# Attention's values by token in four banks, and the fourth tile of the norm turned one step earlier, in a hybrid decoder layer

## The chip, the cores and the metric

One core of a Trainium2 chip runs the whole layer in one launch. The metric is the device time of that launch in microseconds (us). The kernel before was run three times: 647.14, 649.06 and 649.33 us, median 649.06. A further, profiled execution took 649.91 us.

## The reference, cut to what matters

A decoder layer on 512 tokens of width 1024, all in fp32. The input is normed and projected; eight heads of block-sparse attention and eight heads of a chunked delta rule (GDN) run side by side on the projections; both are joined, projected out, normed and added, and a squared-ReLU MLP follows, again normed and added.

```python
h = rms_norm(x, pre_mix_norm[l])
proj = jnp.einsum('bsd,dc->bsc', h, w_in[l])
att_q, att_k, att_v, gdn_qkv, gdn_z, gdn_a, gdn_b = jnp.split(proj, split_points, axis=-1)
o_att = moba_attention(att_q, att_k, att_v, rel_bias)
o_gdn = gated_deltanet(gdn_qkv, gdn_z, gdn_a, gdn_b, ...)
mix = jnp.einsum('bsc,cd->bsd', jnp.concatenate([o_att, o_gdn], axis=-1), w_out[l])
x = x + rms_norm(mix, post_mix_norm[l])
h = rms_norm(x, pre_mlp_norm[l])
m = jnp.einsum('bsf,fd->bsd', jnp.square(jax.nn.relu(jnp.einsum('bsd,df->bsf', h, w_up[l]))), w_down[l])
x = x + rms_norm(m, post_mlp_norm[l])
```

With 512 tokens and blocks of 256, all earlier blocks are selected, so attention is causal softmax over all keys, with a bias by distance.

## The kernel before, in words

**Precision.** Each large product is made as three matmuls of operands split into a high and a low part (`mm3`, L139): high by high, high by low, low by high. The split is a rounding copy on ScalarE and a subtraction on VectorE or GpSimd. Scores times values, the GDN scan and all turns are plain fp32.

**The projections** (`projections`, L247) have 28 items of 128 output columns, in the order of the string `ORDER` (L26): k, q, v, z are GDN's, x, y, w are attention's queries, keys and values of one pair of heads. An item is 8 steps of `mm3` into a bank of the tag `mm` (there are two): weights stand still, the normed input `hT` (features by tokens) moves, 512 columns a matmul. So a result lies with its columns on the partitions and tokens along the free axis. After the last step a stream (`take_k`, `take_q`, `take_v`, `take_z`, `take_a`) takes the bank away. For a value item (`ev_v`, L625) that is a ScalarE copy out of the bank (L627), four turns of 128x128 on TensorE into a bank of the tag `a` (L629, by the helper L83) and a second ScalarE copy (L631), because scores times values wants tokens on the partitions. Weights come in halves of an item, 256 KB each, on SP's queue, two halves ahead.

**The order of the work.** TensorE's order is written by the kernel itself. `Weave` (L29) holds streams, Python generators with a rank. It keeps a clock of its own, `weave.now`, that each matmul advances by a modelled time, and always goes on with the stream of lowest rank that is due. A stream yields either a delay (from the table `WAIT`, L20, in modelled us) or the name of a mark that another stream sets. The projections (rank 5) yield after each `mm3` and so fill what the others leave. On the other engines a list scheduler sets the order by its own model; `LEAD` (L23) is a head start there. On TensorE nothing overtakes: if a matmul's operand is late, all waits.

**Attention** is done by pairs of heads, p = 0 to 3. `scores` (L645) waits for the mark `a{p}` and, after the first pair, for `turned{p-1}`; for four blocks of queries it makes two score banks (tag `a`, of which there are three), VectorE adds the bias and takes the minimum (L669), ScalarE takes the exponential (L671). `values` (L681) turns the probabilities and multiplies them with the pair's values; its last step (L727) scales, and the mark `att{p}` follows. Items x2 and x3 wait for `att0` and `att1`.

**GDN.** `chunks` (L554) makes the matrices of a pair of heads from k and q: `turned` (L512) builds the tile RC (L525 to L527), which `rows` spreads by matmuls. `inverse` (L732) then solves 32x32 triangles on VectorE alone: 31 rounds of a product (L743) and a subtraction (L744). `scan` (rank 3) runs the recurrence once `inverse` and v0 to v3 are done.

**The output** (`output`, L936) multiplies by w_out for four tiles of 128 tokens; the steps of pair 3 come in `second` (needs `att3`). `normed` (L979), one stream a tile, sums squares on ScalarE, scales and adds on VectorE (L992, L993, L998), waits `WAIT["normed"]`, turns the tile in two banks of the tag `a` and splits it (L112, L113). `up0` (rank 7) then multiplies the first columns of w_up, four parts for tokens 0 to 255, waits for `n3`, and four parts for tokens 256 to 511.

**After that** up and down are made with fewer, combined products and a written-out order on all engines. Nothing there is touched.

Large tiles come from the pool `big` with 14 slots; scratch of attention from `at`.

Of the kernel before, what the change touches and what calls it, by code (L numbers as in the profile page):

```python
# [28 lines left out]

class Weave:  # L30
# [35 lines left out]
                self.live.remove(s)  # L66


def layer(ctx, tc, nc, x, w_in, w_ab, w_out, w_up, w_down, conv_w, a_log, dt_bias, gdn_norm_w, rel_bias,
          pre_mix, post_mix, pre_mlp, post_mlp, c_ident, c_mask, c_tri, c_ones, c_sel, c_su, c_hot, out):  # L70
    stt = nc.vector.scalar_tensor_tensor
    tt = nc.vector.tensor_tensor
# [84 lines left out]
    def bank(tag="g", shape=(128, 512)):  # L157
        return psum.tile(list(shape), FT, name="ps_" + tag, tag=tag, bufs={"mm": 2, "g": 3, "a": 3}[tag])
# [7 lines left out]
    def kof(pair, k, cols=slice(0, 512)):  # L166
        return pair[k // 4][:, k % 4, cols]
# [92 lines left out]
    def projections(items):  # L260
        begin = lambda n, at=None: begun(w_in[items[n // 2][0] // 128, :, 4 * (n % 2):4 * (n % 2) + 4], (4, 128), at)
        end = lambda w: ended(w, nc.gpsimd.tensor_tensor)
        load = lambda n: end(begin(n))
        W = first_w
        W += [begin(0), begin(1)]
        yield 0
        w1 = big("w1", dt=FR)
        W += [begin(2 + i, (w1[:, 2 * i], w1[:, 2 * i + 1], nb0[:, 1024 + 512 * i:1536 + 512 * i])) for i in range(2)]
        yield 0
        for i in range(2):  # L270
            W[i] = end(W[i])
# [18 lines left out]
        W = [third, load(5)]  # L290
        for n in range(4, 2 * len(items)):
            col, ev, need = items[n // 2]
            if n % 2 == 0:
                if need:
                    yield need
                ps = bank("mm")
            if n + 2 < 2 * len(items):
                W.append(load(n + 2))
            hi, lo = W.pop(0)
            for j in range(4):  # L300
                k = 4 * (n % 2) + j
                mm3(ps, hi[:, j], lo[:, j], kof(hT_h, k), kof(hT_l, k), k == 0, k == 7)
# [311 lines left out]
    def take_a(p):  # L614
        def ev_q(ps):
            pts[p] = big("pt", dt=FR)
            nc.scalar.mul(pts[p][:, 0], ps, -0.125)
            stt(pts[p][:, 1], ps, -0.125, f32(pts[p][:, 0]), op0=OP.mult, op1=OP.subtract)
            yield 0

        def ev_k(ps):
            split(pts[p][:, 2], pts[p][:, 3], ps)
            yield 0

        def ev_v(ps):  # L625
# [9 lines left out]
        return [(128 * p, ev_q, need), (512 + 128 * p, ev_k, None), (1024 + 128 * p, ev_v, None)]  # L635

# [6 lines left out]
    def scores():  # L643
        for p in range(4):
# [257 lines left out]
    W = {}  # L902
# [78 lines left out]
    def normed(t, P, xs, nb):  # L981
# [48 lines left out]
    def up0():  # L1030
# [458 lines left out]
```

## Time and profile before

| | us |
|---|---|
| median of three runs | 649.06 |
| the profiled execution | 649.91 |
| its span, first to last instruction | 648.1 |
| outside the span | 1.8 |
| TensorE busy | 630.9 |
| VectorE busy | 443.8 |
| ScalarE busy | 361.5 |
| GpSimd busy | 180.6 |

Times in the rows are us from the span's start; "x4" counts merged instructions; what stands in brackets behind a row is idle time of the engine just before, and what ended it. The mean of "one" is its time in the pipeline; the next matmul can start before it ends, so the distance from start to start is what a matmul costs. The stages: norm and first items to about 30 us, projections with GDN and attention to about 270, output product to 320, up to about 490, down to the end.

### The profile page before, as it was taken

The page shows a single profiled execution, that of the slowest core. Times are in us where ns is not written, and L with a number is a line of the kernel's source. Part 1 is how long each engine was busy: PE and PEld are TensorE (multiplying, and loading weights), DVE is VectorE, ACT ScalarE, POOL GpSimd, SP SyncE. Part 2 cuts the span into 40 slices and gives each one's busy share as a digit, 9 for nine tenths or more (in the row PEclk, how much of TensorE's full clock was granted, in tenths as well). Part 3 has the DMA queues.
Part 4 walks back from the last instruction along what each step waited for, and adds up shares of the span by engine and source line. Part 5 has one row for each costly group of instructions (what it writes and reads, how often), then busy time and mean ns, then how long its engine had stood idle before and what let it go on. Part 6 is the DMA issues. An engine that isn't in the chain of part 4 may idle for free.

```text
span 648.1 us, 11158 instructions
## 1 busy us (share of the span) xinstructions
PE 630.9 (97%) x4375; PEld 527.0 (81%) x4375; DVE 443.8 (68%) x619; ACT 361.5 (56%) x614; POOL 180.6 (28%) x219
## 2 busy tenths in 40 slices
PE   7999999999999999999999999999999999999995
PEld 6877787666777777687898899999998888887884
DVE  5357764898522455665755578787879888988776
ACT  6367645264647556744423476656665656665661
POOL 5356475332446334002402311221211130000002
PEclk7999999989999999999999999999999999999999
DMA  7231223323351113561399899989999999757503
GB/s 239 83 100 66 66 88 95 112 81 114 107 105 51 34 45 105 192 231 73 122 357 247 187 287 226 280 239 261 290 223 342 293 292 293 242 199 296 189 1 129
DMA packets 60341, 113.16 MB, mean 175 GB/s; under 512 B 15702, under 2 KB 34777, under 8 KB 59906
## 3 DMA queue, kind: packets, MB, share of 16 engines
q1 hardware_dynamic: 42594, 83.10, 36.8%
q0 software_dynamic: 17696, 29.36, 21.6%
q8 instruction: 34, 0.56, 0.3%
q14 instruction: 17, 0.14, 0.1%
HBM read 106.65 MB, written 35.15 MB: 219 GB/s over the span
## 4 chain that ended last, share of the span: by engine, by line
PE 84%; DVE 7%; DMA 3%; ACT 2%; POOL 1%; issue 1%; SPq 0%; DVEq 0%; POOLq 0%; ACTq 0%
PE ps_mm L79 42%; PE ps_g L79 24%; PE ps_a L79 15%; PE ps_a L83 2%; DVE conv L364 1%; PE ps_g L83 1%; DVE pr L743 1%; DVE inv L744 1%; DMA xx<-in_x 1%; DMA wd<-d_T 1%; POOL by L174 1%; DMA inv<-d_n 0%; DMA w_raw<-in_w_in 0%; DVE ma_l L113 0%; DMA wo_raw<-in_w_out 0%
## 5 line engine op out<-in xcount | busy, mean ns | idle before, releaser
L137 POOL TENSOR_TENSOR w_lo<-w_raw,w_hi 128x512 fp32r<-128x512 f32 x54 | 70.8, 1311 | 103.1 <-ACT w_hi L136 94.1
L79 PE MATMUL ps_mm<-hT_h,w_hi 128*128 128x512 f32 (+1 forms) x224 | 93.8, 419 | 0.4 <-DVE conv L364 0.4
L79 PE MATMUL ps_mm<-hT_l,w_hi 128*128 128x512 f32 (+1 forms) x224 | 87.5, 391 | 0.4 <-DVE hT_l L113 0.4
L79 PE MATMUL ps_mm<-hT_h,w_lo 128*128 128x512 f32 (+1 forms) x224 | 87.3, 390 | 0.0
L112 ACT CAST wdh<-wd 128x1024 fp32r<-128x1024 f32 x53 | 55.9, 1054 | 52.0 <-PE ps_mm L79 23.5
L113 DVE TENSOR_TENSOR u_l<-w,u_h 128x1024 fp32r<-128x1024 f32 x46 | 56.2, 1224 | 36.0 <-ACT u_h L112 35.4
L113 DVE TENSOR_TENSOR wdl<-wd,wdh 128x1024 fp32r<-128x1024 f32 x53 | 64.9, 1225 | 22.8 <-ACT wdh L112 22.7
L112 ACT CAST u_h<-w 128x1024 fp32r<-128x1024 f32 x46 | 47.8, 1047 | 55.6 <-PE ps_a L79 20.7
L1169 POOL DMA_DIRECT2D d_T<-in_w_down x32 | 33.0, 1032 | 144.7 <-DMA d_T<-in_w_down 73.9
L136 ACT CAST w_hi<-w_raw 128x512 fp32r<-128x512 f32 x56 | 34.6, 619 | 40.0 <-PE ps_mm L79 20.9
L79 PEld LDWEIGHTS ps_mm<-hT_h,w_hi 128*128 128x128 f32 x224 | 43.4, 194 | 13.9 <-issue 6.0
L79 PEld LDWEIGHTS ps_mm<-hT_h,w_lo 128*128 128x128 f32 x224 | 43.5, 194 | 9.0
L170 POOL TENSOR_SCALAR s<-s 128x1 f32<-128x1 f32 x12 | 3.8, 316 | 163.9 <-DVE s L1364 107.7
L79 PEld LDWEIGHTS ps_mm<-hT_l,w_hi 128*128 128x128 f32 x224 | 43.6, 195 | 6.8 <-DVE hT_l L113 0.7
L79 PE MATMUL ps_mm<-wdh,u_h 128*128 128x512 f32 x116 | 45.3, 390 | 0.0
L79 PE MATMUL ps_mm<-wdl,u_h 128*128 128x512 f32 x116 | 45.1, 389 | 0.0
L79 PE MATMUL ps_mm<-wdh,u_l 128*128 128x512 f32 x116 | 45.1, 389 | 0.0
L364 DVE SCALAR_TENSOR_TENSOR conv<-ps_mm,cw,conv 128x511 f32<-128x511 f32 (+2 forms) x36 | 26.8, 744 | 12.6 <-ACT conv L361 12.1
L113 DVE TENSOR_TENSOR u_l<-f,u_h 128x1024 fp32r<-128x1024 f32 x28 | 34.1, 1219 | 0.0
L79 PE MATMUL ps_g<-wdh,u_h 128*128 128x512 f32 x80 | 31.2, 390 | 0.4 <-DVE y L1343 0.4
L79 PE MATMUL ps_g<-wdh,u_l 128*128 128x512 f32 x80 | 31.1, 389 | 0.0
L79 PE MATMUL ps_g<-wdl,u_h 128*128 128x512 f32 x80 | 31.1, 389 | 0.0
(434 smaller groups left out, 1728.4 us busy)
## 6 DMA issues: line engine op xcount, KB each, us to landing
d_T<-in_w_down POOLq DMA_DIRECT2D x48, 512.0 KB, 9.8
wd<-d_T SPq DMA_DIRECT2D x32, 512.0 KB, 6.1
w<-in_w_up SPq DMA_DIRECT2D x28, 512.0 KB, 7.2
w_raw<-in_w_in SPq DMA_DIRECT2D x54, 256.0 KB, 2.6
wd<-in_w_down SPq DMA_DIRECT2D x24, 512.0 KB, 7.5
wo_raw<-in_w_out SPq DMA_DIRECT2D x16, 256.0 KB, 2.9
d_T<-d_T POOLq DMA_DIRECT2D x8, 512.0 KB, 11.9
xx<-in_x SPq DMA_DIRECT2D x4, 512.0 KB, 3.3
```

What stands on the lines that cost most here:

```text
L79: nc.tensor.matmul(o, l, r, **kw)
L83: nc.tensor.transpose(o, i, ident[:k, :k])
L112: nc.scalar.copy(hi, src)
L113: tt(lo, src, f32(hi), op=OP.subtract)
L136: nc.scalar.copy(hi, raw)
L137: (sub or tt)(lo, raw, f32(hi), op=OP.subtract)
L170: nc.gpsimd.tensor_scalar(r, ss, 1.0 / n, EPS, op0=OP.mult, op1=OP.add)
L174: nc.gpsimd.tensor_tensor(r, r, m, op=OP.pow)
L364: stt(c[:, s:], p[:, :512 - s], cw[:, ft, j:j + 1], c[:, s:], op0=OP.mult, op1=OP.add)
L743: tt(v, iN[:, 0:m, m:m + 1].to_broadcast([128, m, w]), iU[:, m:m + 1, m:32].to_broadcast([128, m, w]), op=OP.mult)
L744: tt(iU[:, 0:m, m:32], iU[:, 0:m, m:32], v, op=OP.subtract)
L1169: nc.gpsimd.dma_start(d_T[t][k], block(b, second)[k], accum_op=OP.add, max_dma_last_dim=1024)
```

## The change

- The four value items become one: `by_token` (new). The normed input stands still (128 tokens), the values' weights move (512 columns, all eight heads), for each of 8 steps and 4 tiles of tokens one `mm3`, into four banks, `mm`, `mm`, `a`, `g`. The result has tokens on the partitions, so `ev_v` and its turns go; four ScalarE copies fill one `big` tile `VT`, which `values` reads. The weights come as a new input `w_v` of eight pieces of 128x512, by the same queue and the same distance ahead.
- The mark `a{p}` is set by the keys' item, and `values` waits for a mark `v`.
- `ORDER`: the one value item stands after x1 and ahead of v0 to v3; y0 comes four items earlier.
- `normed` has a delay of its own for tile 3 and a `g` bank for the second half of tile 1.
- `WAIT`, `RANK`, `LEAD` and `START` have other numbers.

```diff
-WAIT = {..., 'k': 4.72, 'q': 3.34, 'z': 7.99, 'r_out': 3.96, 'kk': 1.97, 'va': 1.38, 'a': 2.4, 'row': 1.38, 'rows': 3.2, 'att': 1.43, 'p1': 1.88, 'p2': 1.7, 'w': 1.78, 'state': 1.12, 'normed': 11.21, ...}
-RANK = {'chunks': 5, 'inverse': 3, 'scan': 3, 'scores': 5, 'values': 5, 'finish_o': 1, 'take': 4}
-LEAD = {'chunks': 0, 'inverse': 0, 'scan': 100, 'scores': 0, 'values': 100, 'finish_o': 400, 'take': 0, 'take_a': 100}
+WAIT = {..., 'k': 5.19, 'q': 2.1, 'z': 2.87, 'r_out': 4.94, 'kk': 2.44, 'va': 0.5, 'a': 5.28, 'row0': 1.24, 'row': 1.38, 'rows': 5.12, 'att': 1.17, 'p1': 2.8, 'p2': 0.82, 'w': 2.33, 'state': 1.23, 'normed3': 7.6, 'normed': 8.97, ...}
+RANK = {'chunks': 1, 'inverse': 3, 'scan': 3, 'scores': 5, 'values': 5, 'finish_o': 2, 'take': 3}
+LEAD = {'chunks': 0, 'inverse': 100, 'scan': 100, 'scores': 0, 'values': 100, 'finish_o': 0, 'take': 200, 'take_a': 100}
-START = (5.5, 9.0, 17, 16, 33, 10.5)
-ORDER = "k0 q0 x0 k1 k2 q1 q2 k3 z0 q3 y0 x1 v0 w0 v1 y1 w1 v2 v3 x2 y2 w2 x3 y3 z1 w3 z2 z3"
+START = (5.5, 9.0, 17, 16, 30, 16.5)
+ORDER = "k0 q0 x0 k1 q1 q2 y0 k2 k3 z0 q3 x1 w0 v0 v1 v2 v3 y1 x2 y2 x3 y3 z1 z2 z3"
+V_BANKS = "mm mm a g"
...
+    def by_token(W, u, ahead):
+        VT.append(big("V"))
+        ps = [bank(t) for t in V_BANKS.split()]
+        for k in range(8):
+            ahead(u + k)
+            hi, lo = W[u + k]
+            for t in range(4):
+                ts = slice(128 * t, 128 * t + 128)
+                mm3(ps[t], kof(hT_h, k, ts), kof(hT_l, k, ts), hi[:, 0], lo[:, 0], k == 0, k == 7)
+                if k == 7:
+                    nc.scalar.copy(VT[0][:, t], ps[t])
+                yield 0
+        mark("v", WAIT["va"])
...
         def ev_k(ps):
             split(pts[p][:, 2], pts[p][:, 3], ps)
+            mark(f"a{p}", WAIT["a"])
             yield 0
-        def ev_v(ps):
-            v = at.tile([128, 512], FT, name="t2")
-            nc.scalar.copy(v, ps)
-            yield WAIT["va"]
-            tp = transposed(by_tile(v), "a")
-            vals[p] = at.tile([128, 512], FT, name="V")
-            nc.scalar.copy(vals[p], tp)
-            mark(f"a{p}", WAIT["a"])
...
-                yield WAIT["row"]
+                yield WAIT["row" if p else "row0"]
...
             yield f"row{p}3"
-            V = vals[p].rearrange("p (t h e) -> p t h e", t=4, h=2)
+            yield "v"
...
-        yield WAIT["normed"]
+        yield WAIT["normed" if t < 3 else "normed3"]
         for b in range(2):
-            tp = bank("a")
+            tp = bank("g" if t == b == 1 else "a")
```

## Rows read from the trace of the kernel before

**Rows 1.** The page's first part: engine, busy us (share of the span), instructions

```profile
PE 630.9 (97%) x4375; PEld 527.0 (81%) x4375; DVE 443.8 (68%) x619; ACT 361.5 (56%) x614; POOL 180.6 (28%) x219
```

**Rows 2.** Who waited for whom, TensorE: us in total, times, longest

```profile
PE ps_a L79 <- DVE mins L669: 1.8, 1, 1.8
...
PE ps_g L79 <- DVE ssq L382: 0.9, 1, 0.9
PE ps_g L83 <- ACT sqt L378: 0.7, 1, 0.7
...
PE ps_g L79 <- DVE RC L527: 0.5, 1, 0.5
```

**Rows 3.** Windows after the longest wait: busy and count by engine, PEclk, DMA, GB/s

```profile
130.00:132.00 2.00, 1.52 (x6) 1.09 (x7) 2.00 (x8) 1.54 (x4) 0.14 (x1) 0.59 0.02 4
132.00:134.00 2.00, 2.00 (x6) 1.57 (x7) 2.00 (x5) 1.14 (x4) 1.14 (x1) 0.56 0.00 0
```

**Rows 4.** Groups of instructions that go: busy us, mean ns, idle before

```profile
L83 PE MATMUL ps_a<-ident,t 128*128 128x128 f32 x16 | 2.6, 283 | 0.0
...
L631 ACT COPY V<-ps_a 128x512 f32<-128x512 f32 x4 | 2.3, 587 | 3.3 <-PE ps_a L83 3.3
```

**Rows 5.** Timeline of TensorE around four of those turns: start, us, instruction

```profile
153.53 0.66 PE L83 MATMUL ps_a<-ident,t 128*128 128x128 f32 x4
153.94 0.48 PE L79 MATMUL ps_mm<-hT_h,w_hi 128*128 128x512 f32 x1
154.25 0.39 PE L79 MATMUL ps_mm<-hT_l,w_hi 128*128 128x512 f32 x1
```

**Rows 6.** Timeline of TensorE where the down product changes its bank

```profile
510.99 0.39 PE L79 MATMUL ps_g<-wdh,u_l 128*128 128x512 f32 x1
511.22 0.39 PE L79 MATMUL ps_a<-wdh,u_h 128*128 128x512 f32 x1
```

**Rows 7.** The window of those changes, columns as in rows 3

```profile
510.00:520.00 10.00, 10.00 (x46) 8.29 (x45) 8.56 (x8) 6.86 (x8) 3.06 (x4) 1.00 1.01 243
```

**Rows 8.** Timeline at the end of item x1: its last matmul and its two readers

```profile
108.83 0.39 PE L79 MATMUL ps_mm<-hT_h,w_lo 128*128 128x512 f32 x1
...
109.60 0.59 ACT L617 ACTIVATE pt<-ps_mm 128x512 fp32r<-128x512 f32 x1
...
110.22 0.69 DVE L618 SCALAR_TENSOR_TENSOR pt<-ps_mm,pt 128x512 fp32r<-128x512 f32 x1 [1.16 <-ACT pt L617]
```

**Rows 9.** A window among the convolutions, columns as in rows 3

```profile
60.00:80.00 20.00, 18.42 (x118) 14.59 (x116) 15.09 (x27) 13.26 (x36) 8.98 (x11) 1.00 0.25 66
```

**Rows 10.** Group of the widest score operations on VectorE: busy us, mean ns, idle before

```profile
L669 DVE CUSTOM_DVE_ANT_0 L<-ps_a,E 128x512 f32<-128x512 f32 x8 | 5.3, 688 | 14.5 <-PE ps_a L79 14.5
```

**Rows 11.** Timeline of TensorE at the norm's turns and the first up product

```profile
307.35 0.66 PE L83 MATMUL ps_a<-ident,xs 128*128 128x128 f32 x4 [0.59 <-DVE ma_l L113]
...
318.76 0.28 PE L79 MATMUL ps_mm<-ma_h,wu 128*128 128x256 f32 x1
...
331.13 1.04 PE L83 MATMUL ps_a<-ident,xs 128*128 128x128 f32 x8
332.41 0.38 PE L79 MATMUL ps_mm<-ma_h,wu 128*128 128x256 f32 x1 [0.24 <-ACT ma_h L112]
333.13 0.39 PE L79 MATMUL ps_mm<-ma_l,wu 128*128 128x256 f32 x1 [0.34 <-DVE ma_l L113]
```

**Rows 12.** Timeline of VectorE in the norm of tile 2

```profile
311.69 3.58 DVE L137 TENSOR_TENSOR w_lo<-w_raw,w_hi 128x512 fp32r<-128x512 f32 x2 [0.32 <-ACT w_hi L136]
...
318.59 1.28 DVE L998 SCALAR_TENSOR_TENSOR xs<-xs,s,nb 128x1024 f32<-128x1024 f32 x1 [2.19 <-POOL s L174]
```

**Rows 13.** Timeline of TensorE: pair 3's first scores, and where pair 3 is needed

```profile
252.47 0.96 PE L79 MATMUL ps_a<-pt 64*128 64x512 f32 x6
...
291.68 0.39 PE L79 MATMUL ps_mm<-wo_h,ma_h 128*128 128x512 f32 x1
```

**Rows 14.** The pairs' last step on VectorE: ns min/median/max, first and last start

```profile
L727 DVE TENSOR_TENSOR t<-ps_a,t x4: 683/688/692, 154.7 to 275.6; 128x512 f32<-128x512 f32 x4
```

More of the change, by code (lines that the diff above doesn't have):

```diff
@@ L18 @@
 EPS = 1e-6
-WAIT = {'h': 1.7, 'conv_k': 5.5, 'k': 4.72, 'conv_q': 6.15, 'q': 3.34, 'conv_v': 11.0, 'v': 6.02, 'z': 7.99, 'ab': 0.1, 'g': 11.93, 'scalars': 4.6, 'r_in': 0.72, 'r_out': 3.96, 'kk': 1.97, 'kk_out': 14.43, 'gl': 2.12, 'qk': 4.27, 'va': 1.38, 'a': 2.4, 'row': 1.38, 'rows': 3.2, 'pv': 1.54, 'att': 1.43, 'inverse': 0.9, 'merge': 11.0, 'p1': 1.88, 'p2': 1.7, 'w': 1.78, 'vn': 1.0, 'state': 1.12, 'o_in': 3.6, 'o': 3.73, 'wo': 0.88, 'wo_out': 17.6, 'normed': 11.21, 'n': 1.7, 'up': 1.9, 'sums': 1.5, 'turned': 0.5, 'pv0': 1.5}
-RANK = {'chunks': 5, 'inverse': 3, 'scan': 3, 'scores': 5, 'values': 5, 'finish_o': 1, 'take': 4}
-LEAD = {'chunks': 0, 'inverse': 0, 'scan': 100, 'scores': 0, 'values': 100, 'finish_o': 400, 'take': 0, 'take_a': 100}
+WAIT = {'h': 1.7, 'conv_k': 5.5, 'k': 5.19, 'conv_q': 6.15, 'q': 2.1, 'conv_v': 11.0, 'v': 6.02, 'z': 2.87, 'ab': 0.1, 'g': 11.93, 'scalars': 4.76, 'r_in': 0.72, 'r_out': 4.94, 'kk': 2.44, 'kk_out': 14.43, 'gl': 2.75, 'qk': 3.88, 'va': 0.5, 'a': 5.28, 'row0': 1.24, 'row': 1.38, 'rows': 5.12, 'pv': 1.54, 'att': 1.17, 'inverse': 0.9, 'merge': 11.0, 'p1': 2.8, 'p2': 0.82, 'w': 2.33, 'vn': 1.0, 'state': 1.23, 'o_in': 3.6, 'o': 3.73, 'wo': 0.97, 'wo_out': 17.6, 'normed3': 7.6, 'normed': 8.97, 'n': 2.12, 'up': 1.9, 'sums': 1.5, 'turned': 0.5, 'pv0': 1.53}
+RANK = {'chunks': 1, 'inverse': 3, 'scan': 3, 'scores': 5, 'values': 5, 'finish_o': 2, 'take': 3}
+LEAD = {'chunks': 0, 'inverse': 100, 'scan': 100, 'scores': 0, 'values': 100, 'finish_o': 0, 'take': 200, 'take_a': 100}
 FILL = (6, 2)
 AT_X = (3, 5)
-START = (5.5, 9.0, 17, 16, 33, 10.5)
-ORDER = "k0 q0 x0 k1 k2 q1 q2 k3 z0 q3 y0 x1 v0 w0 v1 y1 w1 v2 v3 x2 y2 w2 x3 y3 z1 w3 z2 z3"
+START = (5.5, 9.0, 17, 16, 30, 16.5)
+ORDER = "k0 q0 x0 k1 q1 q2 y0 k2 k3 z0 q3 x1 w0 v0 v1 v2 v3 y1 x2 y2 x3 y3 z1 z2 z3"
+V_BANKS = "mm mm a g"
 class Weave:
@@ L66, in run, with layer @@
                 self.live.remove(s)
-def layer(ctx, tc, nc, x, w_in, w_ab, w_out, w_up, w_down, conv_w, a_log, dt_bias, gdn_norm_w, rel_bias,
+def layer(ctx, tc, nc, x, w_in, w_v, w_ab, w_out, w_up, w_down, conv_w, a_log, dt_bias, gdn_norm_w, rel_bias,
           pre_mix, post_mix, pre_mlp, post_mlp, c_ident, c_mask, c_tri, c_ones, c_sel, c_su, c_hot, out):
@@ L289, in projections, with ahead @@
                 yield 0
[L290 to L302, printed above, removed]
+        units = [(i, m) for i in range(2, len(items)) for m in range(2 if items[i] else 8)]
+        W = [third]
+        def ahead(u):
+            while len(W) < min(len(units), u + 3):
+                i, m = units[len(W)]
+                W.append(load(2 * i + m) if items[i] else wchunk(w_v[m], (1, 512), nc.gpsimd.tensor_tensor))
+        u = 0
+        ahead(-1)
+        for item in items[2:]:
+            if not item:
+                yield from by_token(W, u, ahead)
+                u += 8
+                continue
+            col, ev, need = item
+            if need:
+                yield need
+            ps = bank("mm")
+            for k in range(8):
+                if k % 4 == 0:
+                    ahead(u + k // 4)
+                hi, lo = W[u + k // 4]
+                mm3(ps, hi[:, k % 4], lo[:, k % 4], kof(hT_h, k), kof(hT_l, k), k == 0, k == 7)
                 if k == 7:
@@ L305, in projections @@
                 yield 0
+            u += 2
         mark("projected")
+    VT = []
+    def by_token(W, u, ahead):
+        VT.append(big("V"))
+        ps = [bank(t) for t in V_BANKS.split()]
+        for k in range(8):
+            ahead(u + k)
[7 more added lines that the diff above has]
+        mark("v", WAIT["va"])
     sP = ctx.enter_context(ExitStack())
@@ L601, in layer @@
     d_e = dram.tile([8, 640], FT, name="d_e")
-    pts, vals = {}, {}
+    pts = {}
     def bias():
@@ L702, in product @@
                 for hh in range(2):
-                    mm(po[64 * hh:64 * hh + 64, 128 * k:], V[:, k, hh], P[hh], start=k == 3, stop=k == 0, skip_group_check=True)
+                    mm(po[64 * hh:64 * hh + 64, 128 * k:], VT[0][:, k, 128 * p + 64 * hh:128 * p + 64 * hh + 64], P[hh], start=k == 3, stop=k == 0, skip_group_check=True)
                 weave.now -= (512 - 128 * k) * 4 / 2400
@@ L1049, in layer @@
     take = {"k": take_k, "q": take_q, "v": take_v, "z": take_z, "x": lambda p: take_a(p)[0],
-            "y": lambda p: take_a(p)[1], "w": lambda p: take_a(p)[2]}
+            "y": lambda p: take_a(p)[1], "w": lambda p: None}
     items = [take[n[0]](int(n[1])) for n in ORDER.split()]
@@ L1464, in arrays @@
     return {"x": c(a["x"][0]), "w_in": c(w[:, :, :3584].reshape(8, 128, 28, 128).transpose(2, 1, 0, 3)),
-            "w_ab": c(w[:, :, 3584:].transpose(1, 0, 2)), "w_out": c(a["w_out"][0]), "w_up": c(a["w_up"][0].reshape(2, 4, 128, 16, 256).transpose(3, 0, 2, 1, 4)),
+            "w_v": c(w[:, :, 1024:1536]), "w_ab": c(w[:, :, 3584:].transpose(1, 0, 2)), "w_out": c(a["w_out"][0]), "w_up": c(a["w_up"][0].reshape(2, 4, 128, 16, 256).transpose(3, 0, 2, 1, 4)),
             "w_down": c(a["w_down"][0].reshape(16, 2, 128, 2, 512).transpose(3, 0, 2, 1, 4)),
@@ L1472, in arrays @@
             "pre_mlp": c(a["pre_mlp_norm"][0]), "post_mlp": c(a["post_mlp_norm"][0]), **constants()}
-_NAMES = ["x", "w_in", "w_ab", "w_out", "w_up", "w_down", "conv_w", "a_log", "dt_bias", "gdn_norm_w", "rel_bias",
+_NAMES = ["x", "w_in", "w_v", "w_ab", "w_out", "w_up", "w_down", "conv_w", "a_log", "dt_bias", "gdn_norm_w", "rel_bias",
           "pre_mix", "post_mix", "pre_mlp", "post_mlp", "c_ident", "c_mask", "c_tri", "c_ones", "c_sel", "c_su", "c_hot"]
```

2 lines of the change are left out of this document (1 added, 1 removed).

## The prediction, made before the change was run

> **What bounds the kernel now.** I read the page first, then TensorE's waits, then the windows around the longest wait, then the timeline at each place that the change touches. The page says TensorE: busy 97% of the span, VectorE 68% [rows 1]. What takes work off TensorE, or lets it wait less, shortens the kernel; what the other engines save counts only through a wait. The list of waits is short: between the first items and the up product the longest are 1.8 us for VectorE's score minimum, 0.9 and 0.5 for tiles of `chunks`, 0.7 for a square on ScalarE [rows 2]. The windows show what the longest one brought with it: after it the granted clock was 0.59 and 0.56 in two stretches of 2 us, a mix of TensorE's two levels, 1.2 and 2.4 GHz [rows 3]. So that wait cost more than its 1.8 us. The sum below is made against the profiled execution, 649.91 us (span 648.1, 1.8 outside it); the median of the runs is 649.06, 0.85 lower, and I take that off at the end.
>
> **The change, part by part.**
>
> *The turns that go.* Sixteen turns of 128x128, in four groups, and four ScalarE copies of 0.59 [rows 4]; the other four copies stay as those of the four banks. On the timeline, four turns and the matmul behind them take from 153.53 to 154.25, 0.72 us [rows 5]; that matmul alone is worth 0.23 (154.25 is its successor's start; its spacing: [rows 6]), which leaves 0.49 for a group: **-2.0 us** for four. The copies were beside TensorE's work and are worth nothing by themselves. By the mean duration of a turn, 283 ns, one would get 16 x 0.283 = 4.5 us [rows 4]. The Trainium skill (Perfetto Trace Analysis, Identifying the Most-Contended Engine) says that matmul busy time is a poor measure because matmuls are pipelined, and would look at the share of weight loads, here 81% against 97% [rows 1]; the trace agrees, as the spacing of 0.11 us against 0.283 shows. Counted by busy time the result would be 641.5; I don't use it.
>
> *The product by token.* 96 matmuls of 512 columns stand for 96 matmuls of 512 columns. That another operand stands still, and that the bank changes after every three, I cost at nothing: where the down product changes from one bank to another, the start-to-start distance is 0.23 us, as inside a bank [rows 6], at a granted clock of 1.00 in that window [rows 7]. Eight weight pieces of 256 KB go by SP's queue as eight did, equally far ahead, and eight subtractions by GpSimd; nothing is gained or lost there. New is that the second `mm` bank must be free 0.68 us after x1 ends (three matmuls into the first bank), where an item used to have a whole item's time. x1's last matmul started at 108.83, so the next could start at 109.06 and the fourth at 109.74; x1's bank was read until 110.22 + 0.69 = 110.91 [rows 8]. That is a wait of 1.2 us if nothing else is due on TensorE, none if a stream of lower rank steps in, which happens often since all but the last two yield ahead of the projections: **+0.6**, ends 0 and +1.2. Behind the waiting matmul stands all of TensorE's order.
>
> *Attention moved.* y0 comes four items earlier, and its mark no longer waits for a value item, so pair 0's scores move out of the time in which `inverse` has VectorE, and the value product, which needs no VectorE, takes that place. So the 1.8 us and the clock's share go. Of the clock: 2 x 0.41 + 2 x 0.44 = 1.7 us lost by the two stretches, some 0.3 of it (estimate) while TensorE waited anyway: **-3.2** together. But the scores now fall among the convolutions, where VectorE was 15.09 of 20 us busy [rows 9], with eight score operations of up to 0.69 us that two of the three `a` banks wait for [rows 10]. A score operation held up by one convolution step would delay the next block of queries. Ends: 0, and the same 3.2 again; nearer to the first, since VectorE has a quarter free there and `inverse` had left none (2.00 of 2.00, [rows 3]): **+1.0**. Two loads of the bias for pair 0 and two bias matmuls move up with it on SP's queue and TensorE; nobody waits for either now [rows 2].
>
> *Delays.* `r_out` grows by 0.98, `k` and `kk` by 0.47 each: TensorE comes later to RC and to what hangs behind it, the waits of 0.5 and 0.9 [rows 2]. Ends -1.4 and 0, as other work may now be late instead: **-0.9**. The constants start 6 modelled us later (six loads on SP's queue, five GpSimd copies, one VectorE operation) and are first read when item k0 is done: nothing, and if that cover were gone, one convolution late, under 1 us. Other entries move by about a modelled us or belong to streams that TensorE doesn't wait for [rows 2]: nothing.
>
> *The norm.* The second half of tile 1 waited 0.59 us for an `a` bank [rows 11]; with a `g` bank that goes: **-0.6**. Tile 3 was turned at 331.13, after all four parts of `up0`; eight turns end the issue at about 332.0, and the second matmul behind them started at 333.13, which leaves, with 0.12 for one matmul, 1.0 us of waiting for the split [rows 11]. With a delay of 7.6 against 11.21 (a part is 24 x 256 / 2400 = 2.56 modelled us, tile 2's turns 1.7) it stands before the fourth part, which then covers the split: **-1.0**. But the other tiles' delay falls to 8.97 as well: tile 2 is then turned right after tile 3's product, where `up0` started at 318.76 [rows 11]. Its operand was ready at 318.59 + 1.28 = 319.87 [rows 12], 1.1 us after, and the sixteen turns and the wait of tiles 0 and 1 (16 x 0.11 + 0.59 = 2.4), now ahead of its product, no longer give it time: up to 3.5 us late. Against that, 3.58 us of its chain is VectorE busy with two pieces of w_up between two of its steps [rows 12]; if they fall elsewhere it is in time. Ends 0 and +3.5, nearer to 0 as the whole chain also starts closer to its product: **+1.0**.
>
> **Sum:** -2.0 + 0.6 - 3.2 + 1.0 - 0.9 - 0.6 - 1.0 + 1.0 = -5.1; 649.91 - 5.1 - 0.85 = **644.0 us**.
>
> **Rivals.**
>
> *The waits come back.* The scores cost among the convolutions what they cost beside `inverse`, tile 2 is 3.5 us late, the bank wait is full: -2.0 + 1.2 - 0.9 - 0.6 - 1.0 + 3.5 = +0.2, so 649.3. For it: TensorE's order is fixed, so a delay that is too short is paid in full. Against it: only two waits over 0.7 us come from such a collision now [rows 2]. In the same class: the projections end not with TensorE's work but with the chain q3, `inverse`, `scan`, w_out, whose length the change leaves; then only the norm's terms count, 648.5. Chance 0.27 together.
>
> *Attention's pairs come too late (the other side).* Three pairs now have to pass one after another behind y1, the 21st of 28 items, where the kernel before had started pair 1 ahead of v2. Pair 3 took from 252.47 [rows 13] to 275.6; from pair 0's last step to pair 3's it was 154.7 to 275.6, 40.3 a pair with the pauses [rows 14]. Pair 3 is needed at 291.68 [rows 13], some 5 us sooner now, at 287. With 23.1 a pair, pair 1 must begin by 218; with 30, by 197. Should it begin at 207 and take 30, TensorE stands still for ten us ahead of `second`: 654. For it: `scan`, with its better rank, runs in the same time. Against it: the pauses in the 40.3 are a late w2 and w3, which the change takes away. Chance 0.10.
>
> *The clock falls in the value product.* If changing among four banks after every three matmuls made TensorE pause, the granted clock could fall as it did after the wait [rows 3]; 96 x 0.227 = 21.8 us of work at half the clock takes 21.8 more: 665.8. Against it: changes of bank at full clock and unchanged distance [rows 6, 7]. The Trainium skill (TensorE: Matmul & The Clock Gate, A second HAM failure mode: psum-queue depth-cycling) reports such a swinging clock for a kernel that goes through banks each iteration; that would give this rival's time, and the trace so far disagrees. Chance 0.03.
>
> *The fourth tile doesn't move* (its delay runs out only after the fourth part): 645.0, inside the forecast's own range, 640 to 646.5.
>
> **How the numbers follow.** A measurement of this kernel can tell about 0.5% from no change, 3.25 us: faster is below 645.8, slower above 652.3. The forecast has 0.60, of which 0.03 reach above 645.8. Faster 0.57; same 0.27 + 0.02 = 0.29; slower 0.10 + 0.03 + 0.01 for the forecast's far end = 0.14. The range takes the good ends, -2.0 - 3.2 - 1.4 - 0.6 - 1.0 and the square's 0.7 [rows 2], -8.9 or 640.2, with 1.7 for waits too short to be listed: 638.5. Upward it takes the first rival and the bad ends without the scores' gain, 650.5: 651. It leaves out the two slow rivals and a little below.
>
> **What would show it.** Right: no turns with `t` as operand, 96 matmuls at 0.23 us in four banks at a granted clock of 1.00, no wait for `mins` near `inverse`, no wait for `ma_l` before `up0`'s fifth part, TensorE at the up product five us sooner. Wrong: a wait on x1's `pt` over 1.2, on `mins` among the convolutions, on tile 2's `xs`; a gap before `second`; a clock under 1 in the value product; or the same time at the up product with less TensorE work before it.

## The result and the profile after

The changed kernel takes **652.9 us** (median of 4 runs, 652.2 to 654.3) against 649.2 us of the kernel before in the same session (4 runs, 647.1 to 649.6): ratio 1.0066, 95% interval 1.004 to 1.0093. It is slower by 0.7%, above the range of the forecast and on the other side. The profiled execution took 652.92 us, span 651.1, mean granted clock 0.985 (before: 649.91, 648.1, 0.988). Up to the projections' end its lines are numbered higher than before by 1 to 31 (L79 is L80, L364 is L395, L669 is L692), behind them by 23.

The page's first part of the changed kernel; it answers to [rows 1], with the 16 turns gone:

```profile
PE 629.3 (97%) x4359; PEld 528.7 (81%) x4359; DVE 444.7 (68%) x619; ACT 359.9 (55%) x610; POOL 181.8 (28%) x219
```

Who waited for whom, TensorE, changed kernel (us in total, times, longest); it answers to [rows 2]:

```profile
PE ps_mm L80 <- DVE conv L395: 4.5, 1, 4.5
PE ps_g L80 <- DMA UT<-d_u: 4.2, 2, 3.2
PE ps_a L84 <- DVE xs L1021: 1.1, 2, 0.7
...
PE ps_a L84 <- ACT ph L720: 0.8, 2, 0.5
PE ps_g L84 <- DVE LWQ L592: 0.6, 1, 0.6
```

All waits of [rows 2] have left the list: the score minimum's 1.8 us, 0.9 for `ssq`, 0.7 for `sqt`, 0.5 for RC. Two new ones stand on top. As in [rows 3], the clock falls behind them. Windows of the changed kernel (columns as in [rows 3], PEclk third from the end): the by-token product, then two stretches behind the first new wait and two behind the second:

```profile
110.00:130.00 20.00, 20.00 (x92) 16.52 (x90) 12.68 (x27) 6.13 (x11) 9.55 (x9) 1.00 0.42 119
...
158.00:160.00 2.00, 1.74 (x4) 1.48 (x5) 0.84 (x3) 1.72 (x3) 0.58 (x1) 0.50 0.18 68
160.00:162.00 2.00, 2.00 (x6) 1.52 (x6) 1.93 (x3) 0.00 (x0) 0.70 (x1) 0.50 0.10 34
196.00:198.00 2.00, 1.73 (x65) 1.76 (x67) 0.00 (x0) 0.00 (x0) 0.00 (x0) 0.50 0.13 49
200.00:202.00 2.00, 2.00 (x8) 0.56 (x6) 0.00 (x0) 1.07 (x2) 0.00 (x0) 0.50 0.00 0
```

The by-token product (96 matmuls, 106.65 to about 130, 0.23 us from start to start) runs without a pause and at a granted clock of 1.00; behind each wait TensorE is at 0.50, the lower of its two levels.

**The first wait** is read backward along two queues. Timeline of the changed kernel from the end of v0's product to v3's first matmul (start, us, instruction, idle before it and releaser):

```profile
138.65 0.68 ACT L392 ACTIVATE conv<-ps_mm,cw 128x512 f32<-128x512 f32 x1
...
144.62 0.34 DVE L766 TENSOR_TENSOR pr<-inv 128x175 f32<-128x175 f32 x1
144.88 0.74 DVE L395 SCALAR_TENSOR_TENSOR conv<-ps_mm,cw,conv 128x511 f32<-128x511 f32 x1
...
147.51 0.63 ACT L397 ACTIVATE th<-conv 128x512 f32<-128x512 f32 x1 [4.44 <-DVE conv L395]
...
151.24 0.68 DVE L750 TENSOR_TENSOR t<-ps_a,t 128x512 f32<-128x512 f32 x1
...
151.95 0.62 ACT L113 CAST ma_h<-t 128x512 fp32r<-128x512 f32 x1 [3.30 <-DVE t L750]
...
153.00 0.68 ACT L392 ACTIVATE conv<-ps_mm,cw 128x512 f32<-128x512 f32 x1
...
153.33 0.39 PE L80 MATMUL ps_mm<-hT_h,w_lo 128*128 128x512 f32 x1
158.26 0.77 PE L80 MATMUL ps_mm<-hT_h,w_hi 128*128 128x512 f32 x1 [4.54 <-DVE conv L395]
```

v0's convolution starts on ScalarE at 138.65, but its first VectorE step only at 144.88: rounds of `inverse` stand ahead of it in VectorE's queue. Its `th` then holds ScalarE for 4.44 us, and pair 0's cast `ma_h`, which waits for pair 0's quotient behind more rounds of `inverse`, for another 3.30. v1's convolution stands behind both, so it starts at 153.00, five us after v1's product. v3 needs v1's bank and waits 4.54 us.

**The second wait** comes from memory. Timeline of the changed kernel at the start of `scan`:

```profile
177.74 2.02 SPq L783 DMA_DIRECT2D uap<-d_t  x4
...
186.86 0.55 PE L80 MATMUL ps_a<-pt 64*128 64x128 f32 x6
187.51 1.80 POOL L778 MEMSET UT<- 128x2048 f32 x1 [2.25 <-PE ps_a L80]
...
189.34 4.79 SPq L786 DMA_DIRECT2D UT<-d_u  x4
...
195.03 0.28 PE L80 MATMUL ps_g<-UT,uap 32*32 32x32 f32 x2 [3.19 <-DMA UT<-d_u]
196.27 0.44 PE L80 MATMUL ps_g<-UT,uap 32*32 32x32 f32 x9 [0.96 <-DMA UT<-d_u]
```

The four transfers into `uap` go out at 177.74, those into UT 11.6 us later, though nothing but `inverse` was missing for either. Between them stands the clearing of UT on GpSimd, released by pair 1's last score product on TensorE (186.86, L80 into `ps_a`). UT is a tile of the pool `big`; the new tile V holds one of its 14 slots to the end of attention, so UT gets the one that pair 1's `pt` gives back after its last scores.

### The profile page after: what moved, and what is told of

It reads as the page before. It is cut to its first block, busy times and chain, and to the rows that moved or that the text cites. A ratio compares the mean times of both kernels' runs of the same rounds, so it can differ in the third digit from the quotient of the medians.

```text
span 651.1 us, 11131 instructions
## 1 busy us (share of the span) xinstructions
PE 629.3 (97%) x4359; PEld 528.7 (81%) x4359; DVE 444.7 (68%) x619; ACT 359.9 (55%) x610; POOL 181.8 (28%) x219
## 3 DMA queue, kind: packets, MB, share of 16 engines
HBM read 106.65 MB, written 35.15 MB: 218 GB/s over the span
## 4 chain that ended last, share of the span: by engine, by line
PE 82%; DVE 9%; POOL 2%; DMA 2%; ACT 2%; issue 1%; SPq 1%; DVEq 0%; POOLq 0%; ACTq 0%
PE ps_mm L80 41%; PE ps_g L80 24%; PE ps_a L80 14%; DVE inv L767 2%; DVE pr L766 2%; PE ps_a L84 1%; PE ps_g L84 1%; DMA wo_raw<-in_w_out 1%; DVE conv L395 1%; DMA xx<-in_x 1%; DMA UT<-d_u 1%; POOL w_lo L138 1%; DVE ma_l L114 0%; DVE xs L1021 0%; SPq L786 0%
## 5 line engine op out<-in xcount | busy, mean ns | idle before, releaser
L80 PE MATMUL ps_mm<-hT_h,w_hi 128*128 128x512 f32 (+1 forms) x192 | 79.8, 415 | 4.5 <-DVE conv L395 4.5
L80 PE MATMUL ps_mm<-hT_l,w_hi 128*128 128x512 f32 (+1 forms) x192 | 74.7, 389 | 0.3 <-DVE hT_l L114 0.3
L80 PE MATMUL ps_mm<-hT_h,w_lo 128*128 128x512 f32 (+1 forms) x192 | 74.4, 388 | 0.0
L80 PEld LDWEIGHTS ps_mm<-hT_h,w_hi 128*128 128x128 f32 x192 | 37.0, 193 | 16.8 <-issue 9.9
L80 PE MATMUL ps_mm<-wdh,u_h 128*128 128x512 f32 x116 | 45.3, 390 | 0.0
L80 PE MATMUL ps_mm<-wdh,u_l 128*128 128x512 f32 x116 | 45.1, 389 | 0.0
L80 PE MATMUL ps_mm<-wdl,u_h 128*128 128x512 f32 x116 | 45.1, 389 | 0.0
L80 PEld LDWEIGHTS ps_mm<-hT_h,w_lo 128*128 128x128 f32 x192 | 36.8, 192 | 7.8
L80 PEld LDWEIGHTS ps_mm<-hT_l,w_hi 128*128 128x128 f32 x192 | 37.0, 193 | 6.0 <-DVE hT_l L114 0.6
L692 DVE CUSTOM_DVE_ANT_0 L<-ps_a,E 128x512 f32<-128x512 f32 (+3 forms) x32 | 14.4, 488 | 32.6 <-PE ps_a L80 32.6
L395 DVE SCALAR_TENSOR_TENSOR conv<-ps_mm,cw,conv 128x511 f32<-128x511 f32 (+2 forms) x36 | 26.8, 744 | 11.8 <-ACT conv L392 11.3
L80 PE MATMUL ps_g<-wdh,u_h 128*128 128x512 f32 x80 | 31.2, 390 | 0.4 <-DVE y L1366 0.4
L80 PE MATMUL ps_g<-wdl,u_h 128*128 128x512 f32 x80 | 31.1, 389 | 0.0
```

The source lines that it names most:

```text
L80: nc.tensor.matmul(o, l, r, **kw)
L395: stt(c[:, s:], p[:, :512 - s], cw[:, ft, j:j + 1], c[:, s:], op0=OP.mult, op1=OP.add)
```

## Experiments

"V elsewhere" means this edit of the changed kernel, which gives V memory of its own; all runs but 3 and 10 have it. Every ratio is to the kernel before, timed again beside the run:

```diff
-        VT.append(big("V"))
+        VT.append(at.tile([128, 4, 512], FT, name="V", bufs=1))
```

**1. V elsewhere, alone.**

> The changed kernel with one thing altered: the tile V of the by-token values gets memory of its own instead of a slot of the pool of large tiles. Theory (slot): V takes the last free slot, so the scan's tile UT is cleared on GpSimd only when pair 1's score tile comes free (187.5 us), its transfers go out at 189.3 to 194, and TensorE stands idle for 4.2 us and then runs 10.2 us at half clock. With V elsewhere the clearing comes before 170 us, the scan's two waits for the transfers into UT go, the half-clock stretch at 194 to 204 goes with them, and the time falls by 5 to 9 us, to 644 to 648 us. Rival (chain): the scan was held by the inverse and the pairs anyway, another wait takes the place of the transfers, and the time stays within 1.5 us of 652.9 us. The wait of 4.5 us at 153.6 us stays in both.

648.69 us, ratio to before 0.9998 (0.9981 to 1.0015); the changed kernel stood at 1.0066, so the slot cost **0.7%, 4.4 us**, a little under what was expected. Timeline of this kernel, GpSimd's clearing and SyncE's transfers:

```profile
175.73 1.81 POOL L778 MEMSET UT<- 128x2048 f32 x1
...
178.26 2.69 SPq L786 DMA_DIRECT2D UT<-d_u  x4
```

The clearing waits for nobody and comes 11.8 us earlier, no wait for UT is in the list, and the clock at 194 to 204 us is 1.00. The first wait stays, with 4.6 us.

**2. A quarter of the inverse.** `range(31, 0, -1)` becomes `range(31, 0, -4)` at the rounds' loop, which leaves out 23 of the 31 rounds; with V elsewhere.

> As the run before (V with its own memory), and the inverse does only 8 of its 31 rounds: 23 rounds of the triangular solve on VectorE are left out. Theory (VectorE's queue): the wait of 4.5 us for v0's convolution comes from the inverse's rounds that stand ahead of it and of pair 0's quotient in VectorE's queue; with a quarter of the rounds that wait and the half clock behind it (156.6 to 163.4 us) go, and the time falls by another 5 to 8 us, to about 637 to 642 us. Rival (ScalarE): ScalarE's own queue holds the convolution; the wait stays above 3 us although the rounds are gone, and the time stays above 643 us.

646.71 us, one run. TensorE's waits in this kernel: for a convolution there is none.

```profile
PE ps_mm L80 <- ACT V L335: 2.4, 1, 2.4
```

So the rounds were what v0's and v1's convolutions waited for. But the time lies only 2 us below run 1's median, not 7, and 0.4 us above run 1's own profiled execution (646.32). This execution ran its first 20 us at a granted clock of 0.83, and v0 now waits 2.4 us for the copies out of the by-token banks, which stand on ScalarE behind a cast that waited 6.0 us for a weight transfer. The wait is settled by this run, its price isn't.

**3. The norm's part alone**, in the kernel before: delays 8.97 and 7.6, and bank `g` for tile 1's second half.

> The kernel before with the norm's part of the change alone: delay 8.97 for tiles 0 to 2, 7.6 for tile 3, and tile 1's second half into bank g. The prediction's terms for it: -0.6 (bank), -1.0 (tile 3) and +1.0 (tile 2 earlier), so -0.6 us in all: 648.5 us against 649.2. Rival: the stages from the product out to the product up cost TensorE the same in both kernels (the changed kernel waits 1.1 us for xs there), so the time is within 0.5 us of before, or up to 1 us above it.

647.07 us, ratio 0.998 (0.9968 to 0.9992): 1.3 us faster, with an interval from 0.5 to 2.1. That agrees with the forecast's -0.6 in sign and, within the interval, in size.

**4. The by-token product alone**, in the kernel before (V elsewhere): its order less the w items, with w0 for the product, its delays, ranks and norm.

```diff
-ORDER = "k0 q0 x0 k1 k2 q1 q2 k3 z0 q3 y0 x1 v0 w0 v1 y1 w1 v2 v3 x2 y2 w2 x3 y3 z1 w3 z2 z3"
+ORDER = "k0 q0 x0 k1 k2 q1 q2 k3 z0 q3 y0 x1 w0 v0 v1 y1 v2 v3 x2 y2 x3 y3 z1 z2 z3"
```

> The by-token product alone: the kernel before with the values' product by token in four banks and no turning (V in memory of its own), with the delays, ranks, starting delays and norm of before and its order of work, less the three values' items that go. Theory (product is free): the sixteen turns and their waits go, the product itself costs nothing, so 645 to 648 us if the scores still collide with the inverse as before. Rival (product costs): taking four banks at once and loading the values' weights by GpSimd subtractions holds up the convolutions around it; then 650 us or more, and TensorE waits for a bank in the stretch 110 to 135 us.

667.54 us, ratio 1.0293 (1.0253 to 1.0334): far slower, and in neither of the ways expected. TensorE's waits and ScalarE's timeline in this kernel:

```profile
PE ps_g L84 <- DVE ot L908: 6.9, 1, 6.9
PE ps_a L84 <- ACT ph L720: 6.3, 2, 6.0
PE ps_g L80 <- ACT vn L871: 2.2, 1, 2.2
PE ps_g L80 <- DVE S L882: 1.3, 1, 1.3
PE ps_mm L80 <- DVE pt L649: 1.3, 1, 1.3
```
```profile
152.24 0.63 ACT L397 ACTIVATE th<-conv 128x512 f32<-128x512 f32 x1 [6.22 <-DVE conv L395]
152.78 1.05 ACT L720 COPY ph<-ps_a 128x512 f32<-128x512 f32 x2
```

It is the first wait again, longer: a `th` whose convolution stands behind the whole inverse (its last subtraction starts at 148.66) holds ScalarE for 6.2 us, and pair 0's copies, for which TensorE waits, stand behind it. The rest is lost later, in `scan` and at its end, and was not followed further. At x1 the product waits 1.3 us for a bank (`pt`), the upper end of the forecast's term. So under the old order, delays and ranks the product by token is far from free. How much of its cost the new order takes away, and how much the new delays and ranks, no run tells apart.

**5. v0 and v1 ahead of the by-token product** (V elsewhere).

```diff
-ORDER = "k0 q0 x0 k1 q1 q2 y0 k2 k3 z0 q3 x1 w0 v0 v1 v2 v3 y1 x2 y2 x3 y3 z1 z2 z3"
+ORDER = "k0 q0 x0 k1 q1 q2 y0 k2 k3 z0 q3 x1 v0 v1 w0 v2 v3 y1 x2 y2 x3 y3 z1 z2 z3"
```

> V with its own memory, and in the order of work the products v0 and v1 stand ahead of the by-token product (x1 v0 v1 w0 v2 v3) instead of behind it. Theory (VectorE's queue): v0's and v1's convolutions then come ahead of all but about five of the inverse's 31 rounds, and the by-token product, which asks nothing of VectorE, runs beside the inverse; the wait of 4.5 us for a convolution and the half clock behind it go, and against the run with V's own memory (648.7 us) the time falls by 5 to 8 us, to 641 to 644 us. Rival (the inverse bounds): whatever stands beside the inverse, something waits for its end, and the time stays within 1.5 us of 648.7 us, with a wait of 3 us or more between 140 and 170 us in another place.

650.72 us, ratio 1.0019 (0.9997 to 1.0042): a miss. The wait for the convolution behind the inverse went, and another of 4.8 us came. Timeline of TensorE in this kernel:

```profile
120.87 0.39 PE L80 MATMUL ps_mm<-w_hi,hT_l 128*128 128x512 f32 x1
126.05 0.77 PE L80 MATMUL ps_mm<-w_hi,hT_h 128*128 128x512 f32 x1 [4.79 <-DVE conv L395]
```

The by-token product takes both `mm` banks at once, within 0.7 us, and the second one is v1's, whose product has only just ended. That is the forecast's "second bank" term, with a convolution in place of x1's two short evictions.

**6. Pair 0's values later**: the delay `va` from 0.5 to 6 (V elsewhere).

> V with its own memory, and one delay: pair 0's values may begin 6 us after the by-token product (0.5 us in the changed kernel), which puts the convolutions of v0 and v1 ahead of pair 0's copies and cast in ScalarE's queue, and 3 rounds of the inverse earlier in VectorE's. Theory (both queues: v1's convolution stands behind pair 0's cast on ScalarE, which stands behind the inverse on VectorE): the wait for v1's convolution falls from 4.6 us to 2 us or less, the time to 644 to 647 us. Rival (VectorE alone, v1's convolution is late whatever ScalarE does): the wait stays at 3 us or more, the time at 648 to 650 us.

647.86 us, ratio 0.9975 (0.9955 to 0.9996), a time between the two expectations, and a wait as the rival had it: it moves from v3 to v2, for v0's convolution, and is 3.2 us long (timeline of TensorE):

```profile
146.11 0.75 PE L80 MATMUL ps_mm<-hT_h,w_hi 128*128 128x512 f32 x1 [3.22 <-DVE conv L395]
```

The convolution's first VectorE step comes at 143.4, again behind rounds of the inverse, though nothing holds it on ScalarE, where it starts at 135.4. So most of the wait (3.2 of 4.6 us) stays with VectorE's queue alone.

**7. The values' subtractions on VectorE** (V elsewhere): `wchunk(w_v[m], (1, 512))`, without `nc.gpsimd.tensor_tensor`.

> V with its own memory, and the subtractions that split the values' weights (eight pieces of 128x512 and no others) run on VectorE instead of GpSimd. Theory (GpSimd holds VectorE up): in the changed kernel an inverse operation takes 1.27 to 1.44 us where a GpSimd subtraction runs beside it, and about 0.4 us elsewhere; with those subtractions on VectorE the long inverse operations of that stretch go, each subtraction costs VectorE about 0.6 us, so the inverse ends 2 to 4 us earlier and v1's convolution waits less than 3 us. Rival (the length is the operation's own, or the shared memory's): the inverse's operations stay at 1.3 us in the same number, and the inverse ends later by the subtractions' 5 us.

648.16 us, one run; the wait stays at 4.6. The number of long operations did not fall: the two at the inverse's start (119.5 and 122.6 in run 1) are gone with the values' subtractions, but the inverse, now with other work between its rounds, ends about 3 us later and meets two subtractions of the next items at its end (151.1 and 152.5), so there are eight long operations as before. Inconclusive for the time. For the mechanism see the last section.

**8, 9. v0 ahead of x1** (V elsewhere), and the same with `va` 6.

```diff
-ORDER = "k0 q0 x0 k1 q1 q2 y0 k2 k3 z0 q3 x1 w0 v0 v1 v2 v3 y1 x2 y2 x3 y3 z1 z2 z3"
+ORDER = "k0 q0 x0 k1 q1 q2 y0 k2 k3 z0 q3 v0 x1 w0 v1 v2 v3 y1 x2 y2 x3 y3 z1 z2 z3"
```

> V with its own memory, and the product v0 stands ahead of x1 (v0 x1 w0 v1 v2 v3): v0's convolution is done during x1 and before the inverse begins, and the by-token product takes v0's bank and x1's, of which the second is freed by two short evictions and no convolution. Theory (order): neither the wait of 4.6 us at v3 (changed kernel) nor that of 4.8 us at the by-token product (the run with v0 and v1 both ahead) comes; v1's convolution is late behind the inverse, but its bank is asked for only at about 154 us. Against the run with V's own memory (648.7 us) 4 to 7 us less: 642 to 645 us, faster than before by 0.6 to 1.0%. Rival (the inverse bounds): one of the products behind the inverse still waits 3 us or more for a convolution, and the time stays at 647 to 650 us.

> As v0_before_x1, with pair 0's values 6 us later (delay 0.5 to 6 us), which puts v1's and v2's convolutions ahead of pair 0's cast on ScalarE. If a convolution is still waited for in v0_before_x1, the wait goes here and the time is 1 to 3 us below it; if none is, the two are within 1 us, and pair 0's later values cost nothing, since pair 1 is not begun before the inverse's end.

648.53 us, ratio 0.9997 (0.9976 to 1.0018), and 649.08 us, 1.0001 (0.9982 to 1.0019): two misses. In the first, as the rival had it, y1 waits 4.2 us for v2's convolution. TensorE's longest wait in run 8, and below it ScalarE's timeline, with the same chain one item later:

```profile
PE ps_mm L80 <- DVE conv L395: 4.2, 1, 4.2
...
159.14 0.62 ACT L113 CAST ma_h<-t 128x512 fp32r<-128x512 f32 x1 [3.21 <-DVE t L750]
...
160.19 0.68 ACT L392 ACTIVATE conv<-ps_mm,cw 128x512 f32<-128x512 f32 x1
```

In run 9 the wait for a convolution did not go as expected: it is 3.6 us long, and 2.1 us for pair 0's copies come on top. In both runs, with one value item (v0) ahead of the inverse, something stands behind its rounds.

**10. That order with V in the pool `big`.**

> The changed kernel with the order of v0_before_x1 alone (V stays in the pool of large tiles). Theory (two separate costs): the slot's cost stands by itself, so the scan waits for the transfers into UT by some 4 us and the time is 4 to 6 us above v0_before_x1, 647 to 650 us. Rival (one cost: the late convolutions make pair 1's scores late, and these hold the slot): with the order mended the slot comes free in time, the wait for UT is under 1 us, and the time is within 1.5 us of v0_before_x1.

653.34 us, ratio 1.0072 (1.0049 to 1.0096); 4.8 us above run 8, as the theory had it. The wait for UT is back (TensorE's waits in this kernel):

```profile
PE ps_g L80 <- DMA UT<-d_u: 4.0, 2, 3.0
```

The slot's cost is its own, and about the same as in run 1.

**11, 12. Other banks.** The order of run 5, and the by-token product in banks that no convolution holds; in run 12 also `va` 4.

```diff
-V_BANKS = "mm mm a g"
+V_BANKS = "a g a g"
```

> As order_v_first (V with its own memory; x1 v0 v1 w0 v2 v3), and the by-token product takes the banks a g a g instead of mm mm a g, so it begins without v0's and v1's convolutions. Theory (banks): the 4.8 us that the by-token product waited there were its two mm banks, each held until a convolution is done; with other banks that wait is under 1 us, v0's and v1's convolutions run beside the by-token product, and no product stands behind a convolution that stands behind the inverse by more than 2 us. Against order_v_first (650.7 us) 5 to 8 us less: 643 to 646 us. Rival (the inverse bounds): v2's or v3's convolution behind the inverse is waited for 3 us or more, and the time is 647 to 650 us, as in the other orders with V's own memory.

> As banks_ag, with pair 0's values 4 us after the by-token product, which puts v2's and v3's convolutions ahead of pair 0's cast on ScalarE and of its quotient on VectorE. If banks_ag waits for v2's or v3's convolution, that wait is 1 to 2 us shorter here and so is the time; if not, the two are within 1 us.

Run 11: **643.74 us**, ratio 0.9927 (0.9904 to 0.9951), faster than both kernels. TensorE's longest waits in it:

```profile
PE ps_g L84 <- DVE vB L449: 1.2, 1, 1.2
PE ps_a L84 <- DVE xs L1021: 1.1, 2, 0.7
PE ps_g L80 <- DVE rb L185: 1.1, 1, 1.1
```

No product waits for a convolution, and `scan` doesn't wait for UT. New are 1.2 us for a turn that wants a `g` bank and, as in the other runs with V elsewhere except 4 and 12, 1.0 to 1.5 us within UT's products that the profile ascribes to no other engine. Run 12 is a miss, 652.23 us, ratio 1.0054 (1.0031 to 1.0078). ScalarE and TensorE in its timeline:

```profile
161.80 0.63 ACT L397 ACTIVATE th<-conv 128x512 f32<-128x512 f32 x1 [7.75 <-DVE conv L395]
...
165.57 1.12 PE L84 MATMUL ps_a<-ident,R 128*128 128x128 f32 x4 [6.59 <-ACT ph L720]
```

I had put v2's convolution ahead of pair 0's copies so that it should not wait for them. In VectorE's queue it still stood behind all that were left of the 31 rounds (its first step comes at 159.4, after the last of them), so its `th` held ScalarE for 7.75 us and the copies stood behind that. It is run 4's wait over again.

## Why the prediction was wrong

Starts of TensorE's work at four places, by the timelines of the profiled executions, in us:

| | before | norm alone (3) | changed | V elsewhere (1) | other banks (11) |
|---|---|---|---|---|---|
| `scan`, first product (`uap`, NT) | 190.0 | 187.1 | 188.5 | 186.9 | 183.6 |
| `scan`, first product with UT | 194.4 | 191.5 | 195.0 | 190.2 | 186.9 |
| product out | 271.2 | 268.3 | 276.0 | 269.1 | 267.0 |
| product up | 318.8 | 317.3 | 323.7 | 316.8 | 314.7 |

The table shows where time is lost, not how much a change is worth, for each column is one execution. Run 3 does the same work as the kernel before up to the product out, and yet it is there 2.9 us sooner. Of that, 2.4 us are there when `inverse` begins (112.3 against 114.7), and the first 20 us differ in granted clock (windows, columns as in [rows 3], the kernel before and run 3):

```profile
0.00:20.00 20.00, 16.53 (x85) 14.13 (x86) 9.65 (x22) 10.82 (x21) 10.03 (x23) 0.74 0.69 228
0.00:20.00 20.00, 17.07 (x104) 14.74 (x105) 11.81 (x26) 12.45 (x23) 9.98 (x23) 1.00 0.70 227
```

So the sizes come from the ratios. Mended in V's memory and in the order with its banks, the change is worth 0.73% by run 11, 4.7 us (interval 3.2 to 6.2). The forecast's sum was -5.1. That the two are close tests no single term: only the norm's was run by itself. What the sum lacked are two costs.

- **The turns that go (-2.0), the product by token (0).** The turns are gone from the page; no run measures their -2.0 by itself. The by-token matmuls lost nothing: no wait is listed for them, and their window stands at 20.00 of 20.00 us busy at clock 1.00. The rival in which the clock falls there is refuted. The swinging clock that the Trainium skill (TensorE: Matmul & The Clock Gate, A second HAM failure mode: psum-queue depth-cycling) reports for another kernel did not come here. The second bank's wait (0 to +1.2) did not come in the changed kernel; it was 1.3 us in run 4 and 0.9 in run 8, where x1's `pt` was waited for.
- **The step that failed first is "The product by token"**, where pieces, queues and banks were counted but not where its result lives. V is a new tile of 8 KB a partition in a full pool. The sum has no term for its memory. It cost +4.4 us (run 1) or +4.8 (run 10 against run 8), about the length of the wait for UT itself.
- **The step that failed second is "Attention moved".** It said rightly that the value product asks nothing of VectorE and can stand beside `inverse`, and that the score minimum's wait would go; both are so (for the clock in this term, see the last section). But to put that product there, v0 had been moved from ahead of the w0 item to behind twenty us of by-token product, and v1 with it, so that their convolutions fell beside and behind the inverse. Of the moved items I followed the scores and not the values. The price, from run 1 to run 11, is 0.71% by the ratios, 4.6 us; run 11 changes the order and the banks together, and run 5 shows that the order alone gains nothing.
- **The scores among the convolutions (+1.0)** cost less than that: the changed kernel's list has no wait for `mins`.
- **Delays (-0.9).** The waits for `ssq`, RC and `sqt`, 2.1 us together, are gone; they are back in run 4 with the old delays and order, so delays and order are not told apart here.
- **The norm (-0.6).** Run 3 measured -1.3 (-2.1 to -0.5). The tiles that now come late, put at +1.0, are the two waits for `xs`, 1.1 us together, in run 3 as in the changed kernel; the waits for `ma_l` of [rows 11] are gone.
- **The rivals.** "Attention's pairs come too late" had the right side and the wrong place: in the changed kernel no pair is waited for ahead of the product out. That waits come back in another place was the right family, but what I priced there were the scores and the norm, not the values' convolutions. The end of 650.5 that the range was built on adds up to 650.2 by the forecast's own terms, which changes nothing.

What stays open: run 4's waits behind `scan`, 10 us together, were seen but not taken apart.

## What to carry to other kernels

A tile that outlives its stage takes a slot from whoever allocates next: before costing such a change, list the pool's tiles that are alive together, and look whose memory waits for whose last reader. A product that needs no eviction on a busy engine is good cover, but what it pushes back comes out behind that engine's long task; follow the displaced items' evictions through every in-order queue, where one instruction that waits for the busy engine holds all that stand behind it, even on an engine that is busy for little more than half of the span (ScalarE, 55%). And when a product takes several banks at once, ask who held each of them last: here changing the banks alone was worth 0.9%, 6 us (run 5 to run 11, by their ratios).

## What the hardware showed beyond that

**VectorE stands still beside GpSimd.** VectorE and GpSimd in the changed kernel's timeline, two rounds of the inverse:

```profile
120.04 1.29 POOL L138 TENSOR_TENSOR w_lo<-w_raw,w_hi 128x512 fp32r<-128x512 f32 x1 [1.43 <-ACT w_hi L137]
120.19 1.27 DVE L766 TENSOR_TENSOR pr<-inv 128x112 f32<-128x112 f32 x1
121.50 0.27 DVE L767 TENSOR_TENSOR inv<-inv,pr 128x112 f32<-128x112 f32 x1
...
123.36 1.31 POOL L138 TENSOR_TENSOR w_lo<-w_raw,w_hi 128x512 fp32r<-128x512 f32 x1 [2.03 <-ACT w_hi L137]
123.56 1.31 DVE L767 TENSOR_TENSOR inv<-inv,pr 128x175 f32<-128x175 f32 x1
124.90 0.36 DVE L766 TENSOR_TENSOR pr<-inv 128x192 f32<-128x192 f32 x1
```

An operation of 0.3 us that starts during a GpSimd subtraction ends 0.1 to 0.3 us after it, at 121.46 against 121.33 and at 124.87 against 124.67. Eight of the inverse's operations are stretched so, by about 1 us each; in run 7, whose first subtraction on GpSimd beside the inverse starts at 125.2, none is stretched before. The same stretch has a part in the first wait: pair 0's subtraction `ma_l`, behind which v1's convolution starts on VectorE, takes 1.77 us beside GpSimd there, and 0.69 in run 2. The Trainium skill (SBUF — State Buffer, SBUF: two separate sides) describes a port pair that the two engines share and that one holds for a whole instruction; the trace agrees. What the inverse would cost without it was not measured.

**The same wait does not always cost clock.** The kernel before fell to 0.59 and 0.56 behind its 1.8 us wait [rows 3]; run 3 has that wait too (first line, of TensorE's waits; it ends 2.4 us earlier there), with 1.00 in the same windows and in those just ahead of them, from 126 on:

```profile
PE ps_a L79 <- DVE mins L669: 2.1, 2, 1.8
...
130.00:132.00 2.00, 1.88 (x11) 1.16 (x9) 2.00 (x6) 1.13 (x3) 0.73 (x1) 1.00 0.09 18
132.00:134.00 2.00, 1.97 (x11) 1.22 (x8) 2.00 (x5) 1.72 (x6) 0.40 (x1) 1.00 0.30 113
```

So the forecast's 1.4 us of clock in "Attention moved" belonged to that execution and does not always come with the wait.
